# Hybrid attention step on one core: two local projections run in heads 0 and 1 by way of DRAM, and the modulations move to the same heads

## The chip, the cores and the metric

The kernel runs on one core of a Trainium2 chip. The metric is the device time of one execution in microseconds. A core has TensorE (PE; PEld is its weight load), VectorE (DVE), ScalarE (ACT), GpSimd (POOL) and SyncE (SP), which issues the DMAs here. The engines run beside each other and are ordered by semaphores.

## The reference

Two layers act on 1,024 sample tokens and 128 prompt tokens of width 1,024, here 9 tiles of 128 tokens. Each layer is, cut to what matters:

```python
shift, scale, gate = split(silu(c) @ w_ada + b_ada)      # modulation: three parts of 1024
h = layernorm(x) * (1 + scale) + shift
q, k, v, g_att, f, g_f, u, vm, g_m = split(h @ w_in)     # 4 x 512, then 5 x 256 columns
a = softmax(q1 k1) - lam * softmax(q2 k2)                # 4 heads, 1024 queries, 1152 keys
att = rmsnorm(a @ v) * subln_w * silu(g_att)
four = fft2(f per group of 64) @ w_f * silu(g_f)
gmlp = u * (w_s @ layernorm(vm per head of 64) + b_s) * silu(g_m)
x = layernorm(alpha * x + gate * ([att, four, gmlp] @ w_out)) * ln_g + ln_b
```

The prompt's tokens attend to themselves alone, with modulations of their own; their keys and values are outputs too.

## The kernel before, in words

All matrix products take fp32 operands that are split in a high and a low part, so that each product is three matmuls (high x high, high x low, low x high). The normalized, modulated input H stays in SBUF for a whole layer.

**The attention** (`attention`, `Head`) goes through 4 heads of 8 query blocks of 128. A block has two maps; each takes six score matmuls (line 627), the maximum on VectorE (629) and the exponential on ScalarE (631). `softmax_diff` then scales one map on GpSimd (573) and combines both on VectorE into P (574). One block later TensorE transposes P (641), ScalarE and VectorE split it (644, 645), and once per two blocks TensorE multiplies it by V (651, 27 matmuls). `finish_o` normalizes the result by a matmul of squares (583). `prompt` does the same for the 128 prompt tokens of a head in five small pieces between the steps.

**TensorE's order** is written by hand during the attention (`manual_schedule` for PE): the attention is a generator that yields after each piece, and at each yield `fill.fill(FILL[h] * SHARE[step])` takes projection work off a `Stream` until the given debt is used up. Three projection matmuls of 384 columns count 486, two of 256 columns count 218. `fill.until` takes whole projections at once where a head needs them. The other engines' instructions, and all after the attention, are ordered by a planner from the order of the program, with free buffers; work of low priority may run ahead.

**The stream** holds, in this order: the 16 units of the four heads (K, V, Q, G each; 128 columns by 24 x 3 matmuls of 384 tokens, `mm_dims`, line 375), of which each loads the next one's weights when its first chunk is done; then `local_vm`, `local_u` (u and g_m) and `local_f`, with 256 columns token by token (`mm_tok`, lines 390 and 395). `local_vm` normalizes its result in place: statistics per token and head (778, 779), a power on GpSimd (781), and 36 scalings a layer (785). What the stream still holds at the end of the attention is done at once; then the projection g_f runs beside `local_gmlp` and `fourier_prepare`, followed by `local_fourier` and `out_proj`.

**The modulations** (`mods`): a part multiplies 8 weight tiles with the condition's values and sums up in two accumulators, on VectorE (185, 190) and for three products on ScalarE and GpSimd (187, 188); 8 matmuls sum over the partitions (196). Layer 0's own shift and scale come before its attention. Beside layer 0's attention run its gate and layer 1's shift and scale, beside layer 1's its gate, by `extra.fill(MFILL)` at each step of heads 2 and 3; a part yields nine times 1,000.

**Buffers.** `W` has three tiles for split weights; `wr` two raw tiles that weights and modulations share; `z` three for rotated projections and the like; `mm` two PSUM banks for projections and prompt pieces; `S` two groups of three banks for scores, transposes and values.

## Time and profile before

| | us |
|---|---|
| median of 3 runs (lowest, highest) | 1443.29 (1438.05, 1448.58) |
| the profiled execution | 1441.99 |
| its span | 1440.1 |
| PE busy | 1339.8 (93%) |
| PEld busy | 1234.9 (86%) |
| DVE busy | 908.6 (63%) |
| POOL busy | 794.7 (55%) |
| ACT busy | 746.5 (52%) |

The mean granted clock is 0.982 of full speed. The span runs from the first to the last instruction. Busy times are sums over the span; TensorE's matmuls are pipelined, with modelled ends. DMA moves 114.43 MB, 79 GB/s over the span. In layer 0 the attention goes from 102 to 571 us, in layer 1 from 808 to 1258 us.

### The profile page before, as it was taken

How to read it: one execution, taken by the hardware profiler on the slowest of the kernel's cores; microseconds unless marked ns; L12 is line 12 of the kernel's file. 1: busy time of each engine (PE TensorE's matmuls, PEld its weight loads, DVE VectorE, ACT ScalarE, POOL GpSimd, SP SyncE). 2: the span in 40 equal slices, each digit the busy share in tenths (PEclk: the TensorE clock that was granted, in tenths of full speed). 3: DMA queues.
4: the chain of work that ended last, by engine and by line, in shares of the span. 5: the costliest groups of instructions: out<-in, count | busy, mean ns of one | idle time of the engine just before them, and what ended most of it. 6: DMA issues, size and time to landing. Idle time of an engine off the chain costs nothing. (4 is left out here: it accounts for less than half of the span.)

```text
span 1440.1 us, 21257 instructions
## 1 busy us (share of the span) xinstructions
PE 1339.8 (93%) x8248; PEld 1234.9 (86%) x8248; DVE 908.6 (63%) x1351; ACT 746.5 (52%) x1380; POOL 794.7 (55%) x723
## 2 busy tenths in 40 slices
PE   7899998889899899999998989989799999999997
PEld 3688998879689899987888989988789999998786
DVE  5446667786877856345785565668775684435576
ACT  3466566556454345353565665665565544435320
POOL 3275667576563445236777675575674343533752
PEclk9999999999999999999999999999999999999999
DMA  9310011211221221354341100112110010126432
GB/s 340 142 34 31 19 34 49 76 61 32 87 66 32 88 66 56 100 191 149 124 151 54 51 20 31 48 37 88 32 58 10 30 47 30 42 80 224 152 130 84
DMA packets 56157, 114.43 MB, mean 79 GB/s; under 512 B 4972, under 2 KB 32492, under 8 KB 55928
## 3 DMA queue, kind: packets, MB, share of 16 engines
q1 hardware_dynamic: 56056, 113.07, 23.7%
q8 instruction: 65, 1.06, 0.3%
q14 instruction: 36, 0.29, 0.1%
HBM read 95.47 MB, written 17.58 MB: 79 GB/s over the span
## 5 line engine op out<-in xcount | busy, mean ns | idle before, releaser
L375 PE MATMUL z<-H,w 128*128 128x384 f32 x2520 | 498.7, 344 | 25.5 <-DVE V L495 5.8
L375 PEld LDWEIGHTS z<-H,w 128*128 128x128 f32 x2520 | 443.1, 192 | 32.5 <-ACT vT L481 4.9
L631 ACT ACTIVATE P<-S,nm 128x1152 f32<-128x1152 f32 x128 | 156.4, 1222 | 121.2 <-DVE nm L629 114.5
L629 DVE TENSOR_REDUCE nm<-S 128x1 f32<-128x1152 f32 x128 | 172.3, 1349 | 41.6 <-PE S L627 40.8
L390 PE MATMUL zt<-whi,H 128*128 128x256 f32 x1152 | 158.9, 286 | 5.8 <-ACT ug L756 4.3
L390 PEld LDWEIGHTS zt<-whi,H 128*128 128x128 f32 x1152 | 147.2, 192 | 8.5 <-ACT ug L756 5.0
L573 POOL TENSOR_SCALAR P<-P,rz,neglam 128x1152 f32<-128x1152 f32 x64 | 86.8, 1356 | 101.8 <-DVE rz L572 90.4
L574 DVE SCALAR_TENSOR_TENSOR P<-P,rz 128x1152 f32<-128x1152 f32 x64 | 105.0, 1641 | 42.6 <-POOL P L573 42.6
L619 POOL TENSOR_TENSOR qlo<-qr,Q 64x128 fp32r<-64x128 f32 x128 | 81.5, 642 | 85.8 <-PE S L627 80.2
L356 POOL TENSOR_TENSOR w<-wraw,w 128x1024 fp32r<-128x1024 f32 x36 | 89.6, 2490 | 65.0 <-ACT w L355 64.3
L627 PE MATMUL S<-K,Q 128*128 128x384 f32 x384 | 93.7, 353 | 20.0 <-DVE a L645 9.3
L651 PE MATMUL pv<-a,V 128*128 128x256 f32 x864 | 109.3, 283 | 3.1 <-ACT P L631 3.1
L651 PEld LDWEIGHTS pv<-a,V 128*128 128x128 f32 x864 | 106.5, 191 | 5.1 <-ACT P L631 5.1
L645 DVE TENSOR_TENSOR a<-T,a 128x1152 fp32r<-128x1152 f32 x64 | 86.6, 1352 | 38.1 <-ACT a L644 38.0
L627 PEld LDWEIGHTS S<-K,Q 128*128 128x128 f32 x384 | 68.0, 195 | 28.5 <-DVE a L645 10.9
L627 PE MATMUL S<-K,qlo 128*128 128x384 f32 x384 | 90.1, 343 | 0.0
L1002 PE MATMUL y<-wob,mx 128*128 128x512 f32 (+1 forms) x342 | 87.0, 381 | 1.9 <-DVE rr L1004 1.9
L644 ACT ACTIVATE a<-T 128x1152 fp32r<-128x1152 f32 x64 | 72.3, 1130 | 28.7 <-PE T L641 28.4
L395 PE MATMUL zt<-wlo,H 128*128 128x256 f32 x576 | 82.7, 284 | 1.1 <-POOL wlo L356 1.1
L1002 PE MATMUL y<-wo,mx 128*128 128x512 f32 (+1 forms) x342 | 80.5, 378 | 0.0
L641 PE MATMUL T<-cs,P 128*128 128x128 f32 x576 | 73.6, 273 | 3.8 <-ACT P L631 3.8
L395 PEld LDWEIGHTS zt<-wlo,H 128*128 128x128 f32 x576 | 75.0, 191 | 1.5 <-POOL wlo L356 1.5
(219 smaller groups left out, 2388.3 us busy)
## 6 DMA issues: line engine op xcount, KB each, us to landing
wraw<-in_w_in_dram SPq DMA_DIRECT2D x52, 512.0 KB, 3.3
wada<-in_w_ada_dram SPq DMA_DIRECT2D x32, 512.0 KB, 3.6
wa<-in_w_ada_dram SPq DMA_DIRECT2D x8, 1024.0 KB, 12.3
woraw<-in_w_out_dram SPq DMA_DIRECT2D x16, 512.0 KB, 3.9
mr<-mix SPq DMA_DIRECT2D x18, 384.0 KB, 3.3
mix<-gs SPq DMA_DIRECT2D x8, 576.0 KB, 3.9
x<-rr SPq DMA_DIRECT2D x9, 512.0 KB, 3.3
xr<-x SPq DMA_DIRECT2D x9, 512.0 KB, 5.2
```

Of the source, the lines that this page charges most:

```text
L356: eng.tensor_tensor(lo, raw, f(hi), op=ALU.subtract)
L375: pe.matmul(z, lhsT=w[:, a, kt, :], rhs=Hc[c][:, b, kt, :], start=n == 0, stop=n == 23)
L390: pe.matmul(z[:, i, :], lhsT=Hc[c][:, a, kt, o:o + 128], rhs=w[0][:, kt, :], start=n == 0, stop=False)
L395: pe.matmul(z[:, i, :], lhsT=Hc[c][:, 0, kt, o:o + 128], rhs=w[1][:, kt, :], start=False, stop=kt == KT - 1)
L573: pool.tensor_scalar(p2, p2, rz[:, 1:2], neglam[:, l:l + 1], op0=ALU.mult, op1=ALU.mult)
L574: return dve.scalar_tensor_tensor(p1, p1, rz[:, 0:1], p2, op0=ALU.mult, op1=ALU.add)
L627: pe.matmul(S[:, n, :CH], lhsT=q, rhs=K[:, m, n * CH:(n + 1) * CH], start=e == 0, stop=e == 1)
L629: dve.tensor_reduce(nm, S[:, :, :CH], axis=AX.XY, op=ALU.max, negate=True)
L631: act.activation(P.rearrange("p (c k) -> p c k", c=3), S[:, :, :CH], AF.Exp, bias=nm, accum_out=zz[:, m:m + 1])
L645: dve.tensor_tensor(lo, T[:, :, 0:3], f(hi), op=ALU.subtract)
L651: pe.matmul(pv[:, 0, :], lhsT=self.V[:, a, kt, :], rhs=self.A[:, b, kt, :], start=kt == 0 and e == 0, stop=kt == 8 and e == 2)
L1002: pe.matmul(z, lhsT=mx[:, a, k, :], rhs=wo[kt][b][:, ns], start=i == 0, stop=i == 23)
```

## The change

The stream gets another order: `local_f` stands behind head 1's K, V and Q, `local_vm` behind head 2's, and `local_u` is last. The results of f and of vm, the latter normalized, are stored to DRAM from small tiles of the `z` buffers, and two new steps load them behind the last unit, into the tiles where they were computed before. Weights are loaded ahead only as far as the unit before f or vm; f and vm, their own weights loaded, ask for the unit behind them. FILL has other values. The modulations' steps lie in heads 0 and 1 instead of 2 and 3, and what is left of them is done at head 2's first step. The prompt's sum of squares gets a PSUM bank of its own.

```diff
-MHEAD = 2
-MFILL = 450
+MHEADS = (0, 1)
+MFILL = 480
...
-FILL = [1600, 1500, 1500, 2950]
+FILL = [2450, 2450, 1600, 1700]
...
-X_TAGS = {..., "z": (..., "Pp", "modacc"), ...
+X_TAGS = {..., "z": (..., "Pp", "modacc", "vg", "fg"), ...
...
+    f_d = [dr.tile([128, NT, 256], F32, name=f"f_{l}") for l in range(L)]
+    vm_d = [dr.tile([128, NT, 256], F32, name=f"vm_{l}") for l in range(L)]
...
-        def gen(self, which, together=False, chunks=(0, 1, 2)):
+        def gen(self, which, together=False, chunks=(0, 1, 2), ahead=99):
...
-                            self.load_to(g[-1] + 1)
+                            self.load_to(min(g[-1] + 1, ahead))
...
-            pv = psM((128, 2, 128), "pvp")
-            pe.matmul(pv[:, 0], lhsT=self.vp, rhs=aT, start=True, stop=True)
-            sq = square_o(pv[:, 0], 128)
+            pv = psM((128, 128), "pvp")
+            pe.matmul(pv, lhsT=self.vp, rhs=aT, start=True, stop=True)
+            sq = square_o(pv, 128)
             yield 0.5 * PACE
-            finish_o(l, pv[:, 0], pv[:, 1], sq, 128, self.gs, slice(SEQ_S, TOK))
+            finish_o(l, pv, psM((128, 128), "msp"), sq, 128, self.gs, slice(SEQ_S, TOK))
...
-    def local_vm(l):
-        vm = res["vm", l] = tB("K", [128, NT, 256], "vm", F32)
+    def local_vm(l, then):
         w = load_w256(l, U_VM)
+        then()
         for ts in TG:
             z = yield from mm_tok(w, ts)
             n = len(ts) * H
-            v = vm[:, ts[0]:ts[-1] + 1]
+            v = tX([128, 2, 256], "vg")[:, :len(ts)]
             act.activation(v, z, AF.Copy)
...
-
-    def local_f(l):
+            sp.dma_start(vm_d[l][:, ts[0]:ts[-1] + 1], v)
+
+    def load_vm(l):
+        vm = res["vm", l] = tB("K", [128, NT, 256], "vm", F32)
+        sp.dma_start(vm, vm_d[l])
+        yield 0
+
+    def load_f(l):
         ff = [tX((128, 4, 256), "ff") for _ in range(2)]
         fp = [small([128, 128], n, 2) for n in ("vp", "kp")]
+        for i in range(2):
+            sp.dma_start(ff[i], f_d[l][:, 4 * i:4 * i + 4])
+            sp.dma_start(fp[i], f_d[l][:, 8, i * 128:(i + 1) * 128])
         res["f", l] = ff, fp
+        yield 0
+
+    def local_f(l, then):
         w = load_w256(l, U_F)
+        then()
         for ts in TG:
             z = yield from mm_tok(w, ts)
-            t = ts[0] % 4
-            if ts[0] == 8:
-                for j in range(2):
-                    act.activation(fp[j], z[:, 0, j * 128:(j + 1) * 128], AF.Copy)
-            else:
-                act.activation(ff[ts[0] // 4][:, t:t + 2], z, AF.Copy)
+            fg = tX([128, 2, 256], "fg")[:, :len(ts)]
+            act.activation(fg, z, AF.Copy)
+            sp.dma_start(f_d[l][:, ts[0]:ts[-1] + 1], fg)
...
-        fill = Stream(proj.gen(range(0, 3), together=True, chunks=(0, 1, 2) if l else (2,)), proj.gen(range(3, 4 * H)),
-                      local_vm(l), local_u(l), local_f(l))
+        fill = Stream(proj.gen(range(0, 3), together=True, chunks=(0, 1, 2) if l else (2,)),
+                      proj.gen(range(3, 7), ahead=6), local_f(l, lambda: proj.load_to(7)),
+                      proj.gen(range(7, 11), ahead=10), local_vm(l, lambda: proj.load_to(11)),
+                      proj.gen(range(11, 4 * H)), load_vm(l), load_f(l), local_u(l))
...
                 fill.fill(FILL[h] * SHARE[step])
-                if h >= MHEAD:
+                if h in MHEADS:
                     extra.fill(MFILL)
+                else:
+                    extra.drain()
```

## Rows read from the trace of the kernel before

**Rows 1.** Page, part 1: busy time and share of the span of each engine

```profile
PE 1339.8 (93%) x8248; PEld 1234.9 (86%) x8248; DVE 908.6 (63%) x1351; ACT 746.5 (52%) x1380; POOL 794.7 (55%) x723
```

**Rows 2.** Windows cut by head: length, PE, PEld, DVE, ACT, POOL busy, PEclk, DMA, GB/s

```profile
102.03:196.80 94.77, 90.43 (x554) 87.35 (x554) 60.52 (x74) 57.12 (x111) 60.37 (x63) 0.98 0.09 31
196.80:300.26 103.46, 94.94 (x591) 91.82 (x591) 75.03 (x87) 63.95 (x122) 65.84 (x65) 0.98 0.20 60
300.26:416.84 116.58, 102.24 (x600) 94.90 (x600) 87.75 (x94) 66.16 (x124) 72.17 (x69) 0.96 0.18 58
416.84:571.00 154.16, 146.33 (x1095) 141.59 (x1094) 111.41 (x204) 72.61 (x126) 74.79 (x60) 0.98 0.19 60
571.00:808.30 237.30, 226.03 (x1214) 198.69 (x1213) 131.54 (x213) 123.45 (x236) 149.06 (x117) 0.99 0.37 122
808.30:903.00 94.70, 90.36 (x553) 87.25 (x552) 60.57 (x74) 57.12 (x111) 60.30 (x63) 0.98 0.10 31
903.00:1006.50 103.50, 95.08 (x592) 91.80 (x592) 75.04 (x88) 63.92 (x122) 65.97 (x65) 0.98 0.19 60
1006.50:1115.40 108.90, 98.45 (x600) 92.48 (x599) 73.45 (x85) 63.60 (x122) 67.30 (x69) 0.98 0.10 33
1115.40:1258.20 142.80, 138.79 (x1079) 137.41 (x1078) 87.26 (x185) 69.30 (x123) 59.36 (x55) 1.00 0.11 35
1258.20:1440.10 181.90, 170.45 (x945) 150.76 (x943) 102.09 (x156) 59.77 (x99) 80.45 (x61) 0.99 0.39 134
```

**Rows 3.** Chain of waits in layer 1: start us, us, what

```profile
1037.76 1.04 PE S L627 x6
...
1072.24 3.59 PE mres L196 x8
...
1094.94 2.08 PE z L375 x12
...
1146.57 0.96 PE zt L395 x8
```

**Rows 4.** Timeline of PE, layer 1's head 1: start us, us, ..., [idle before]

```profile
957.44 0.45 PE L674 MATMUL atp<-cs,Pp 128*128 128x128 f32 x1 [2.31 <-DVE rz L572]
...
978.50 0.81 PE L627 MATMUL S<-K,Q 128*128 128x384 f32 x3 [2.45 <-ACT msq L587]
```

**Rows 5.** Groups by line, modulations: busy, mean ns, idle before

```profile
L185 DVE TENSOR_SCALAR macc<-wada,csil 128x1024 f32<-128x1024 f32 x8 | 5.7, 746 | 1.4 <-DMA wada<-in_w_ada_dram 1.2 <-PE mres L196 0.2
...
L187 ACT ACTIVATE wada<-wada,csil 128x1024 f32<-128x1024 f32 x12 | 13.8, 1151 | 9.0 <-DVE macc L190 8.7 <-issue 0.3
...
L188 POOL TENSOR_TENSOR macc<-macc,wada 128x1024 f32<-128x1024 f32 x12 | 29.9, 2489 | 5.8 <-ACT wada L187 5.8
...
L190 DVE SCALAR_TENSOR_TENSOR macc<-wada,csil,macc 128x1024 f32<-128x1024 f32 x44 | 67.3, 1551 | 10.8 <-DMA wada<-in_w_ada_dram 10.6
```

**Rows 6.** Groups by line, the normalization of vm

```profile
L778 DVE BATCH_NORM_STATS2 b<-vm 128x6 f32<-128x64 f32 x72 | 10.7, 206 | 4.8 <-ACT vm L773 4.8
...
L785 DVE TENSOR_SCALAR vm<-vm,mvv,rsv 128x64 f32<-128x64 f32 x72 | 24.5, 411 | 3.0 <-POOL rsv L781 3.0
```

**Rows 7.** Timeline, layer 1's head 2

```profile
1020.14 2.35 POOL L188 TENSOR_TENSOR macc<-macc,wada 128x1024 f32<-128x1024 f32 x1
...
1020.21 3.49 DVE L574 SCALAR_TENSOR_TENSOR P<-P,rz 128x1152 f32<-128x1152 f32 x1 [1.69 <-POOL P L573]
...
1025.02 0.95 PE L627 MATMUL S<-K,Q 128*128 128x384 f32 x3 [4.74 <-DVE a L645]
```

**Rows 8.** Line 574: duration ns min/median/max

```profile
L574 DVE SCALAR_TENSOR_TENSOR P<-P,rz x64: 1379/1419/3540, 111.7 to 1240.0; 128x1152 f32<-128x1152 f32 x64
```

**Rows 9.** DMA issues: KB each, median us to landing

```profile
mix<-gs SPq DMA_DIRECT2D x8, 576.0 KB, 3.9
```

**Rows 10.** Timeline of DVE behind layer 1's attention

```profile
1260.78 2.88 DVE L834 TENSOR_TENSOR vr<-vm,vr 128x1152 fp32r<-128x1152 f32 x1 [2.37 <-ACT vr L833]
```

More of the change, by code (lines that the diff above doesn't have):

```diff
@@ L44 @@
 NEARLY = 6
-FILL = [1600, 1500, 1500, 2950]
+FILL = [2450, 2450, 1600, 1700]
 U_Q, U_K, U_V, U_G, U_F, U_GF, U_U, U_VM, U_GM = 0, 4, 8, 12, 16, 18, 20, 22, 24
-X_TAGS = {"wr": ("wraw", "woraw", "wada", "tabr", "mr", "ba"), "z": ("zz", "sh", "gt", "vT", "gmt", "gmg", "fot", "vs", "bd", "pqp", "ws", "kc", "vc", "Pp", "modacc"), "Q": ("Q", "bdr", "wsr", "h32"),
+X_TAGS = {"wr": ("wraw", "woraw", "wada", "tabr", "mr", "ba"), "z": ("zz", "sh", "gt", "vT", "gmt", "gmg", "fot", "vs", "bd", "pqp", "ws", "kc", "vc", "Pp", "modacc", "vg", "fg"), "Q": ("Q", "bdr", "wsr", "h32"),
           "sq": ("sq", "wft", "dftp", "msq", "bds", "cb")}
```

## The prediction

> **What bounds the kernel now.** I read the page's busy times first, then the busy time cut at the first score matmul of each head, then the chain and the engines' own order inside two heads. TensorE is busy 93% of the span and no other engine more than 63% [rows 1]: only time that TensorE loses can be won. The cut shows where. What a head loses I take as length minus PE busy, plus (1 - PEclk) x length: the granted clock has two levels, 2.4 GHz and half of it, so 0.98 over a window means that 2% of its length was lost at the low level. By that sum layer 0's heads lose 6.2, 10.6, 19.0 and 10.9 us, layer 1's 6.2, 10.5, 12.6 and 4.0; together 46.7 and 33.3 us, 80 in all [rows 2]. The stages between and behind the attentions (237.3 and 181.9 us) run nearly dense.
>
> Two patterns matter. Without modulations, loss falls as projection work per step grows: 10.5 us in head 1 (FILL 1500), 4.0 in layer 1's head 3 (2950). With modulations it rises: layer 0's head 2 loses 8.4 more than its head 1, head 3 loses 6.9 more than layer 1's, and layer 1's head 2 loses 2.1 more than its head 1 [rows 2]. That is 15.3 us for three parts and 2.1 for one.
>
> **The prices of TensorE's work.** From the chain: 12 projection matmuls of 384 columns take 2.08 us (0.173 each), 8 of the token-major ones 0.96 (0.12 each), the six score matmuls 1.04, the eight that close a modulation part 3.59 [rows 3]. None of these counts changes. What changes is their order, so the whole effect is in lost time.
>
> **The projections.** f and vm are 9 tokens x 24 matmuls x 0.12 = 25.9 us each per layer. Counted from the yields, a head has 26, 28, 28 and 30 shares of FILL. Before, that hands out 41.6, 42.0, 42.0 and 88.5 thousand; after, 63.7, 68.6, 44.8 and 51.0. Following the generators, 158 token-major matmuls of f and 200 of f and vm enter heads 0 and 1, the rest of vm lies in head 2, and head 3 keeps G3 and u. Behind the attention 70 matmuls remain instead of 158: 10.6 us of TensorE work move ahead of its end.
>
> What head 1 loses shows what the longer steps are worth: 2.31 us before the prompt's transpose, which waits for VectorE's reciprocal, 2.45 before a score matmul that waits for a bank still read by ScalarE [rows 4]. A step of fill precedes each, and it grows by some 1 us. So at 2450 head 1's loss lies between 4.0 (the 2950 row) and 10.5 (the 1500 row); 2950 is nearer, and I take 5.0. Head 0: 6.2 becomes 3.0 by the same ratio. Head 2 at 1600 keeps 9.5 of 10.5. Head 3 at 1700 goes from 4.0 to 9.0, just under the 1500 row: the gain of two heads is mostly paid back there. Together 26.5 a layer against 6.2 + 10.5 + 10.5 + 4.0 = 31.2.
>
> **The modulations.** One part is 2 starts of 0.75, 11 VectorE multiply-adds of 1.55 (together 18.5 us), and three ScalarE products with GpSimd adds of 2.49 [rows 5]. The step's share (480 against 450) hardly changes the pace: a part takes 17 steps, its closing matmuls stand in TensorE's order at the 17th step, the 36th, and the start of head 2. VectorE is busy 60.5 + 75.0 us in layer 0's heads 0 and 1 [rows 2], some 14 of it already modulation work run ahead (two starts and eight multiply-adds lie before head 2); with three parts (57 with their last adds) and two thirds of vm's normalization (for both layers 24.5 scaling and 10.7 statistics, with the short aggregates about 20 a layer [rows 6]) it has some 192 us in about 250, or 77%, where layer 0's head 2 now has 75%. So VectorE is as full as where the loss is greatest, but the steps are half as long again. The bounds per part are 2.1 (layer 1) and 5.1 (15.3 / 3); I take 4.0 for each of layer 0's three, and 2.1 in layer 1. If a closing matmul finds the sums late, the attention's matmuls stand behind it, for TensorE's order is fixed.
>
> One row speaks against the move. While a GpSimd add of a modulation ran (2.35 us), VectorE's P took 3.49 us and the next score matmul waited 4.74 [rows 7]; P's shortest is 1.38 and its median 1.42 [rows 8]. The Trainium skill has the rule, in Advanced Engine Details and Errata, GPSIMD Details: the Pool engine shares a read and a write interface with VectorE and conflicts with its instructions of two SBUF inputs. The trace agrees, 3.49 us against 1.42. By the rule each of the twelve adds can hold P by 2.07 us, 25 us in all, where my sum holds 14.1 for everything that the parts do; that is the first rival.
>
> **DRAM.** Each layer gains ten stores and five loads on SP's queue: 9 x 128 x 256 floats twice out and back, 4.7 MB. The nearest row, a 576 KB store, lands in 3.9 us [rows 9], and the data are wanted a head or more later. A store waits for ScalarE or the scaling, and weight loads queue behind it; they are issued a unit ahead. Between 0 and +4 us a layer, taken 0. The scratch tiles take one or two of three shared buffers while no unit is rotating: 0 to +3, taken 0. Loading no further than the unit before f or vm could expose one load each (0 to +4); the 26 us of f and vm cover the next unit's. The evacuations are the same operations.
>
> **The prompt's second bank.** The sum-of-squares matmul now needs a second bank of a pair that a projection shares, so it waits until VectorE has read the first. In exchange that read no longer follows the matmul. Between are a step of fill and VectorE's longest instruction shown, 3.49 us [rows 7]: once per head, from about -1 to +1.7; taken 0.
>
> **The end of the attention.** The 8.4 us of projection that remain must cover the splitting of vm, which after layer 1's attention ended (1258.2) ran until 1263.66 [rows 10], 5.5 us. That still fits; what no longer fits are u's last gate chain and slower loads. 0 to +5 a layer, taken +1.
>
> **The sum.** Layer 0: 26.5 + 12.0 = 38.5 against 46.7, -8.2. Layer 1: 26.5 + 2.1 = 28.6 against 33.3, -4.7. Ends +2. Together -11 us from the profiled execution's 1441.99, or 1431; that execution stood 1.3 under the median, so **1432**.
>
> **Rivals.**
> *The modulations collide (slower).* In layer 0's heads 0 and 1 GpSimd is busy 64% before anything is added [rows 2], and three parts in two heads meet the softmax more often. If each add holds P by 2.07 us on TensorE's path, and the last product and add (1.15 + 2.40) stand before the closing matmuls, a part costs 9.8 instead of my mean 3.5. Four make 39 against 14, so +25: 1457. It breaks even near 6.3 a part. Against it: longer steps absorb a 2 us delay that a 1500 step did not. Chance 0.20.
>
> *Longer steps close the gaps (a larger gain).* Head 0 at 1600 loses 6.2, head 1 at 1500 loses 10.5 [rows 2]. If that is a knee and not only head 0's fewer steps, heads 2 and 3 lose 6.5 and 6.0, heads 0 and 1 2.0 and 4.0, and a part 2.1: layer 0 24.8, layer 1 20.6, and with the ends -33: 1410. Against it: head 0 has no older head's values in its first steps. Chance 0.26.
>
> *Loss only moves.* If it falls on a straight line from 10.5 at 1500 to 4.0 at 2950, the heads give 28.3 instead of 31.2 a layer, the parts cost what they did (17.4), and the ends take 2: -4, 1439. Chance 0.12.
>
> **How the numbers follow.** The forecast has 0.42, with its own range 1422 to 1442 from the bounds above. One per cent, about what can be told from no change here, is 14.4 us: below 1429 is faster. A third of the forecast's chance lies there, 0.15, and with the larger gain 0.41 is faster; the rest, 0.27, and the moved loss give 0.39 the same; 0.20 slower. The range 1409 to 1454 takes in the larger gain's own figure and most of the collision.
>
> **What would show it.** Layer 0's heads should last 118, 133, 115 and 107 us (before 94.8, 103.5, 116.6, 154.2), layer 1's 116, 122, 112 and 107, each stage behind an attention about 10 us less. The prompt's wait should be under 1.5 us in heads 0 and 1. P above 3 us beside a modulation add, with score matmuls waiting over 4 us there, would show the first rival; closing matmuls that wait for the sums likewise. Heads 2 and 3 under 7 us of loss would show the second. The forecast is wrong if head 3's loss stays near 4, or if heads 0 and 1 lose over 12 in layer 1, where one part runs.

## The result: 2.5% slower, and where the time stands in the profile after

The changed kernel takes 1477.65 us (median of 4 runs, 1475.95 to 1479.98) against 1443.56 for the kernel before on the same chip: ratio 1.0249, 95% interval 1.0223 to 1.0275 (the two medians by themselves give 1.0236, inside it). The forecast was 1432, with a range up to 1454. The profiled execution took 1475.95 with a span of 1474.2, 34.1 more than the span of before. The mean granted clock is 0.972 (0.982 before).

The page's busy times, as in [rows 1]: the work is the same (8,248 matmuls), but PE's time rose by 8.4 us, while the mean granted clock fell from 0.982 to 0.972.

```profile
PE 1348.2 (91%) x8248; PEld 1240.8 (84%) x8248; DVE 912.6 (62%) x1351; ACT 745.4 (51%) x1378; POOL 793.7 (54%) x723
```

The windows of the kernel after, cut as in [rows 2] (length, then PE, PEld, DVE, ACT and POOL busy, PEclk, DMA share, GB/s): layer 0's four heads, the stage behind its attention, then the same for layer 1.

```profile
103.61:231.41 127.80, 115.03 (x716) 108.62 (x715) 91.65 (x99) 65.51 (x123) 79.54 (x67) 0.96 0.25 78
231.41:369.50 138.09, 123.37 (x807) 116.99 (x808) 99.86 (x142) 72.71 (x133) 84.62 (x73) 0.98 0.24 76
369.50:486.99 117.49, 108.83 (x686) 102.59 (x684) 78.91 (x151) 62.53 (x118) 66.39 (x69) 0.99 0.17 59
486.99:589.32 102.33, 99.22 (x747) 97.56 (x747) 59.21 (x66) 58.01 (x105) 42.41 (x44) 1.00 0.10 33
589.32:827.35 238.03, 216.02 (x1097) 189.95 (x1096) 139.18 (x216) 124.60 (x238) 151.93 (x120) 0.95 0.36 118
827.35:952.39 125.04, 114.33 (x717) 108.42 (x716) 79.78 (x90) 65.09 (x124) 72.31 (x66) 0.96 0.20 65
952.39:1073.60 121.21, 116.16 (x792) 114.38 (x791) 67.91 (x126) 65.53 (x125) 66.40 (x69) 1.00 0.14 46
1073.60:1184.67 111.07, 103.35 (x669) 99.71 (x668) 74.22 (x143) 62.40 (x118) 64.32 (x69) 1.00 0.14 48
1184.67:1288.23 103.56, 99.56 (x747) 97.66 (x747) 61.40 (x66) 58.11 (x105) 42.09 (x44) 1.00 0.10 32
1288.23:1474.17 185.94, 165.51 (x844) 144.37 (x843) 110.46 (x158) 60.84 (x102) 83.05 (x64) 0.94 0.38 129
```

A stage's length has to be set against the work that moved. Per layer 100 token-major matmuls left the stage behind the attention and entered the heads, 100 x 0.12 = 12.0 us [rows 3]; in layer 0 the closing of one modulation part moved the same way (3.6 us and its transposes, some 4).

| | before | after | change | work moved | lost time: change | forecast |
|---|---|---|---|---|---|---|
| up to the attention | 102.0 | 103.6 | +1.6 | 0 | +1.6 | 0 |
| layer 0, heads | 469.0 | 485.7 | +16.7 | +16.0 | +0.7 | -8.2 |
| layer 1, heads | 449.9 | 460.9 | +11.0 | +12.0 | -1.0 | -4.7 |
| layer 0, stage behind | 237.3 | 238.0 | +0.7 | -16.0 | +16.7 | +1 |
| layer 1, stage behind | 181.9 | 185.9 | +4.0 | -12.0 | +16.0 | +1 |

The heads only miss the gain that was forecast, 12.9 us; the loss is not there, where the prediction looked for gain and for harm. Each stage behind an attention has 12 to 16 us less to do and is no shorter: TensorE's idle time there went from 11.3 to 22.0 and from 11.5 to 20.4, and PEclk from 0.99 to 0.95 and 0.94, so part of what is left runs at the low level (1.2 GHz): PE is busy 6.0 and 7.1 us longer there than the moved work leaves.

**What holds the stage.** The timeline of the kernel after, behind layer 1's attention (end 1288.23). Columns: start, duration, engine and line, what ended the idle time. `ug` is u, multiplied by its gate, `ws` the raw spatial weights of gmlp, `wsr` their split, `sg` gmlp's products, `taba` the next table.

```profile
1300.54 1.24 DVE L408 TENSOR_TENSOR gmg<-zt,gmt 128x512 f32<-128x512 f32 x2
...
1301.31 1.29 POOL L766 TENSOR_TENSOR ug<-ug,gmg 128x512 f32<-128x512 f32 x1 [1.14 <-DVE gmg L408]
...
1302.62 0.81 SPq L821 DMA_DIRECT2D ws<-in_wsT_dram  x1
1304.87 0.74 POOL L766 TENSOR_TENSOR ug<-ug,gmg 128x256 f32<-128x256 f32 x1
...
1305.63 0.33 SPq L821 DMA_DIRECT2D ws<-in_wsT_dram  x1
...
1309.33 0.74 POOL L846 TENSOR_TENSOR wsr<-ws,wsr 128x256 fp32r<-128x256 f32 x1 [2.56 <-ACT wsr L845]
1309.57 0.68 PE L832 MATMUL sg<-vr,wsr 128*128 128x320 f32 x4
...
1330.57 0.52 PE L832 MATMUL sg<-vr,wsr 128*128 128x256 f32 x3
...
1331.13 2.01 ACT L845 ACTIVATE taba<-tabr 128x1024 fp32r<-128x1024 f32 x2 [1.71 <-PE sg L832]
```

This is a hand-over of buffers. The multiply of u's gate ends at 1302.60, and the load of `ws` is issued at 1302.62; the next ends at 1305.61, and the second load goes at 1305.63. `ws` and the gate's temporaries (gmt, gmg) share the three `z` buffers. So the load goes out 14.4 us after the attention's end, the products run from 21.3 to 42.9 us after it, and only when they have read `vr` (the split of vm) is the buffer free that `taba` shares with it.

The same places in the kernel before, whose attention ended at 1258.22:

```profile
1251.22 0.37 SPq L809 DMA_DIRECT2D ws<-in_wsT_dram  x1
...
1300.67 0.52 PE L820 MATMUL sg<-vr,wsr 128*128 128x256 f32 x3
...
1301.23 2.01 ACT L833 ACTIVATE taba<-tabr 128x1024 fp32r<-128x1024 f32 x2 [1.02 <-PE sg L820]
```

There u stood ahead of f: its gate was done early, `ws` was loaded 7.0 us before the attention's end, and what the products waited for was the projection that was still to do. `taba` started 43.0 us behind the attention before and 42.9 after; from there to the end it takes 138.9 us before and 143.0 after. The remainder shrank, and the load that f used to cover came out from under it. That the load is the cause, and not only late, is tested by a_ws below.

### The profile page after: what moved, and what is told of

The parts are those of the page before. It is cut to its first block, busy times and chain, and to the rows that moved or that the text cites. A ratio compares the mean times of both kernels' runs of the same rounds, so it can differ in the third digit from the quotient of the medians.

```text
span 1474.2 us, 21366 instructions
## 1 busy us (share of the span) xinstructions
PE 1348.2 (91%) x8248; PEld 1240.8 (84%) x8248; DVE 912.6 (62%) x1351; ACT 745.4 (51%) x1378; POOL 793.7 (54%) x723
## 4 chain that ended last, share of the span: by engine, by line
PE 49%; DVE 19%; ACT 9%; POOL 7%; DMA 6%; issue 5%; SPq 0%; DVEq 0%; POOLq 0%; ACTq 0%
PE z L377 16%; PE y L1014 9%; PE zt L392 5%; PE S L629 5%; PE pv L653 5%; DVE macc L192 4%; ACT P L633 3%; PE zt L397 3%; PE T L643 3%; DVE nm L631 2%; DMA wada<-in_w_ada_dram 2%; DVE P L576 2%; DMA woraw<-in_w_out_dram 2%; POOL K L431 1%; POOL P L575 1%
## 5 line engine op out<-in xcount | busy, mean ns | idle before, releaser
L377 PEld LDWEIGHTS z<-H,w 128*128 128x128 f32 x2520 | 447.1, 194 | 53.2 <-ACT Pp L671 23.6
L631 DVE TENSOR_REDUCE nm<-S 128x1 f32<-128x1152 f32 x128 | 172.7, 1350 | 32.7 <-PE S L629 32.1
L653 PEld LDWEIGHTS pv<-a,V 128*128 128x128 f32 x864 | 106.4, 191 | 11.6 <-ACT P L633 8.3
L629 PE MATMUL S<-K,Q 128*128 128x384 f32 x384 | 90.6, 344 | 10.3 <-DVE a L647 4.3
L192 DVE SCALAR_TENSOR_TENSOR macc<-wada,csil,macc 128x1024 f32<-128x1024 f32 x44 | 69.6, 1605 | 15.8 <-DMA wada<-in_w_ada_dram 15.8
L629 PEld LDWEIGHTS S<-K,Q 128*128 128x128 f32 x384 | 65.8, 190 | 14.4 <-DVE a L647 6.3
## 6 DMA issues: line engine op xcount, KB each, us to landing
wa<-in_w_ada_dram SPq DMA_DIRECT2D x8, 1024.0 KB, 10.7
```

What stands on the lines that cost most here:

```text
L192: dve.scalar_tensor_tensor(acc[c], w, k, acc[c], op0=ALU.mult, op1=ALU.add)
L377: pe.matmul(z, lhsT=w[:, a, kt, :], rhs=Hc[c][:, b, kt, :], start=n == 0, stop=n == 23)
L629: pe.matmul(S[:, n, :CH], lhsT=q, rhs=K[:, m, n * CH:(n + 1) * CH], start=e == 0, stop=e == 1)
L631: dve.tensor_reduce(nm, S[:, :, :CH], axis=AX.XY, op=ALU.max, negate=True)
L653: pe.matmul(pv[:, 0, :], lhsT=self.V[:, a, kt, :], rhs=self.A[:, b, kt, :], start=kt == 0 and e == 0, stop=kt == 8 and e == 2)
```

## The experiments

Where an expectation names a theory by a letter, it is one of these. **A**: behind the attention there is a fixed chain, so work done earlier is never given back. **A2**: u is last, so its gate is wanted at once. **B**: the modulations beside the softmax cost the time. **C**: DRAM and the stream's order. **D**: the shorter remainder uncovers a fixed chain. **E**: g_f's projection stands in TensorE's order ahead of gmlp's products. **F**: the load of `ws` waits for `z` buffers that u's gate holds. **G**: the products' results wait for the gate itself. **H**: longer steps close nothing.

All runs at a glance (ratio to the kernel before on the same chip):

| run | median us | ratio, 95% interval |
|---|---|---|
| b_tail3300n | 1438.55 | 0.9993 (0.9974 to 1.0013) |
| a_tail1350 | 1473.19 | 1.0216 (1.0187 to 1.0246) |
| a_tail2250 | 1476.62 | 1.0253 (1.0226 to 1.0280) |
| a_flast | 1476.44 | 1.0246 (1.0221 to 1.0272) |
| a_gf_late | 1474.24 | 1.0224 (1.0189 to 1.0259) |
| a_ws | 1450.29 | 1.0087 (1.0064 to 1.0111) |
| a_mods23 | 1471.04 | 1.0209 (1.0190 to 1.0228) |
| b_mods01 | 1455.26 | 1.0103 (1.0082 to 1.0124) |
| a_flast_mods23 | 1464.76 | 1.0166 (1.0129 to 1.0203) |
| b_best | 1448.23 | 1.0066 (1.0047 to 1.0086) |
| b_mod1 | 1408.64 | 0.9791 (0.9761 to 0.9821) |
| a_mod1 | 1434.52 | 0.9966 (0.9946 to 0.9986) |
| a_ws_mod1 | 1415.55 | 0.9830 (0.9803 to 0.9856) |
| b_nopool | 1433.54 | 0.9927 (0.9898 to 0.9956) |
| b_tail_nopool | 1431.05 | 0.9917 (0.9893 to 0.9942) |
| a_nopool | 1455.93 | 1.0105 (1.0068 to 1.0142) |
| a_ws_mods23 | 1458.53 | 1.0111 (1.0085 to 1.0138) |
| a_ws_nopool | 1444.68 | 1.0027 (1.0013 to 1.0042) |

### The stage behind the attention

**b_tail3300n**: the kernel before, with as little left behind the attention as after the change.

```diff
-FILL = [1600, 1500, 1500, 2950]
+FILL = [1600, 1500, 1500, 3300]
-MFILL = 450
+MFILL = 520
```

> The kernel before with FILL 3300 in head 3 instead of 2950 (and MFILL 520 instead of 450, so that the last modulation still ends before f begins). Counted from the yields, 62 matmuls of f remain behind the attention instead of 158, 11.5 us per layer, and nothing else moves. Theory A (the stage behind the attention is bound by a chain that starts when the attention ends, so work taken out of it shortens it by nothing): both attentions 11 us longer, the stages behind them as long as before (237 and 182 us, within 3), in all 1443 + 20 = 1463. Theory B (the modulations in the heads of the dense softmax cost the time): no change, 1440 to 1447. Theory C (the DRAM loads and the new order of the stream delay what follows the attention): no change either, since neither is here.

Measured: the same time. The windows of its two stages:

```profile
585.10:804.22 219.12, 208.31 (x1103) 184.75 (x1103) 130.49 (x210) 120.41 (x232) 145.10 (x115) 0.99 0.36 125
1263.22:1434.12 170.90, 159.03 (x850) 139.45 (x849) 104.55 (x155) 57.34 (x96) 79.41 (x60) 0.99 0.41 140
```

With 90 token-major matmuls left instead of 184 the stages are 18.2 and 11.0 us shorter than [rows 2], and PEclk stays at 0.99. The 11.0 is the price of the matmuls (94 x 0.12 = 11.3); in layer 0 the closing of a modulation part moved ahead too, with MFILL at 520. A remainder of this size uncovers nothing by itself: A and D fall. What differs from the changed kernel is what the remainder holds, f here and u there; here `ws` went out 21.2 us before the end of layer 1's attention.

**a_tail1350** and **a_tail2250**: the changed kernel with more of u left behind the attention (176 matmuls), and with nothing left.

```diff
-FILL = [2450, 2450, 1600, 1700]
+FILL = [2450, 2450, 1600, 1350]     # a_tail1350; 2250 in a_tail2250
```

> The changed kernel with FILL 1350 in head 3 instead of 1700: 166 matmuls of g_m remain behind the attention instead of 70, as many as the kernel before had of f. Theory A: head 3 is 11 us shorter in each layer, the stages behind keep their 238 and 186 us within 3, in all 1478 - 21 = 1457. Theory B: no change, 1478, each stage behind 11 us longer. Theory C: no change, or slower.

> The changed kernel with FILL 2250 in head 3 instead of 1700, so that nothing of u remains behind the attention. Theory A2: head 3 grows by the 70 matmuls that moved, some 9 us a layer, and the stages behind shrink by 15 to 20, as the gate is ready when they begin: 1455 to 1465. Theory D: the stages stay at 238 and 186 and the heads grow: 1495. Theory B: about 1478.

Neither moves the time by more than half a per cent. But the two show the coupling: at 1350 the load of `ws` goes out 23.4 us behind layer 1's attention, the last product starts at 50.0 and the stage lasts 188.4; at 2250 they are -12.1, 30.0 and 167.8. At 1350 both loads of `ws` again go out at the end of a gate multiply (23.4 and 26.5). At 2250 the stages are 16.6 and 18.1 us shorter, as A2 had it, for 10 us of work; but PE still idles 23.6 and 19.0 us there, so an early load alone does not make a stage dense when nothing is left to cover it. The heads pay the gain back: layer 1's head 3 lasts 119.7 instead of 103.6, 16 us for 10 us of work moved in.

**a_gf_late**: the products' order against g_f's.

```diff
-        fill.fill(1000)
         while fill.gens:
-            post.fill(700)
+            post.fill(1400)
             fill.fill(1500)
```

> The changed kernel with the projection of g_f given out half as fast beside the gmlp products (no 1000 at first, 1400 of the gmlp's steps for 1500 of the projection). Theory A2: the products wait for u's gate, not for their turn: the stages behind the attention 0 to 4 us shorter, 1470 to 1478. Theory E (the projection of g_f stands in front of the gmlp products in TensorE's order): 10 to 15 us shorter each, 1450 to 1458.

The last product now starts 33.6 us behind layer 1's attention instead of 42.6 and `taba` at 34.0, but g_f's projection ends later (51.7 instead of 44.6) and the first DFT product comes at 51.5 instead of 44.5: stages of 234.5 and 184.7, no gain that can be told. E falls as the cause.

**a_flast**: f last and in its own tiles, as before; only vm goes by way of DRAM.

```diff
...                                                 # local_f as in the kernel before
+                      proj.gen(range(3, 11), ahead=10), local_vm(l, lambda: proj.load_to(11)),
+                      proj.gen(range(11, 4 * H)), load_vm(l), local_u(l), local_f(l))
```

> The changed kernel with f alone put back to the end of the stream and into its tiles, without DRAM; vm, the modulations, the prompt's bank and FILL stay as changed. Some 70 matmuls still remain behind the attention, of f instead of u's gate. Theory A2 (what the stream ends with decides: u's gate is wanted at once by the gmlp products, f only later, so with u last the stage behind the attention begins with a wait for the gate, and cover is used up early): the stages behind the attention fall to 219 and 171 us, as with FILL 3300 in the kernel before, the heads stay within 6 us in sum, in all 1444. Theory B (the modulations beside the softmax): 1470 to 1478. Theory D (the shorter remainder uncovers a fixed chain, whatever the remainder is): 1472 to 1480, stages of 238 and 186.

The total did not move, and I had taken that as evidence against u's place until the stages were read: `ws` goes out 9.9 us before the attention's end, PE's idle time there falls from 22.0 and 20.4 to 13.3 and 11.6 us, and the stages (233.5 and 182.4, with 176 matmuls left) are as dense as before. The heads lost it again: with 11 us less work a layer in them they last 7.2 us longer over both layers, and layer 0's head 1 takes 151.5 us with 18.6 idle; why is open. Two effects cancelled in one number.

**a_ws**: one name moved from one pool of buffers to another, nothing else.

```diff
-..."z": (..., "vs", "bd", "pqp", "ws", "kc", ...), ... "sq": ("sq", "wft", "dftp", "msq", "bds", "cb")}
+..."z": (..., "vs", "bd", "pqp", "kc", ...), ... "sq": ("sq", "wft", "dftp", "msq", "bds", "cb", "ws")}
```

> The changed kernel with the gmlp's raw weights (ws) in the three buffers of sq instead of the three of z, and nothing else. Theory F (with u last, its gate's temporaries hold all z buffers, so the load of ws is issued only 14 us behind the attention and the gmlp products start at 21): ws is issued by 5 us, the products start at 11 to 15 us and end 7 to 10 us earlier, and both stages behind the attention are shorter by that: 1458 to 1464. Theory G (the products' results wait for the gate itself, whose last multiplication starts 16.6 us behind the attention): at most 4 us a stage, 1470 to 1478.

Measured: 1450.29, ratio 1.0087; of the 2.5% that the change cost, 1.6 are gone (23 us). The windows of its two stages, and the timeline behind layer 1's attention, which ends at 1277.65:

```profile
592.08:817.13 225.05, 209.67 (x1097) 185.71 (x1096) 135.88 (x216) 124.41 (x238) 151.25 (x120) 0.98 0.37 125
1277.65:1452.29 174.64, 161.20 (x844) 141.09 (x843) 107.08 (x158) 60.28 (x102) 83.58 (x64) 0.97 0.40 137
```

```profile
1280.60 0.38 SPq L821 DMA_DIRECT2D ws<-in_wsT_dram  x1
...
1288.23 0.69 PE L832 MATMUL sg<-vr,wsr 128*128 128x320 f32 x4
...
1309.76 0.52 PE L832 MATMUL sg<-vr,wsr 128*128 128x256 f32 x3
...
1310.39 2.00 ACT L845 ACTIVATE taba<-tabr 128x1024 fp32r<-128x1024 f32 x2
```

The load goes out 2.9 us behind the attention instead of 14.4, `taba` starts at 32.7 instead of 42.9, and the stages are 13.0 and 11.3 us shorter with the same work, more than the 7 to 10 that F had expected. F is shown. G, which allowed 4 us a stage, falls.

### The modulations

**b_mods01** puts them alone where the change puts them; **a_mods23** and **a_flast_mods23** put them back in the changed kernel and in a_flast.

```diff
-                if h >= MHEAD:                    # b_mods01, MFILL 480
+                if h in (0, 1):
                     extra.fill(MFILL)
+                else:
+                    extra.drain()
```

```diff
-MHEADS = (0, 1)                                    # a_mods23; MFILL 480 in a_flast_mods23
-MFILL = 480
+MHEADS = (2, 3)
+MFILL = 450
-                else:
-                    extra.drain()
-    ... load_vm(l), load_f(l), local_u(l))         # a_mods23 only
+    ... load_vm(l), local_u(l), load_f(l))
```

> The kernel before with the modulations alone moved, to heads 0 and 1 at 480 a step. Theory B: 20 to 35 us slower, 1463 to 1478, layer 0's heads 0 and 1 longer by that. Theory A: 1438 to 1452, heads 0 and 1 longer by 10 to 20 us and heads 2 and 3 shorter by 10 to 15.

> The changed kernel with the modulations back in heads 2 and 3 at 450 a step (f is then loaded behind u, since both want the same buffers). Theory B: 20 to 35 us faster, 1443 to 1458, heads 0 shorter by 10 in both layers. Theory A: heads 0 and 1 shorter, heads 2 and 3 longer by as much: within 8 us of 1478, the stages behind as long as in the changed kernel; and in layer 1, where a single part moves, the 5 us wait of head 0 for the prompt's exponential stays.

> As the changed kernel with f last, and the modulations back in heads 2 and 3 at 480 a step. Theory A2: stages of 219 and 171 us; the modulations' place is worth 4 to 8 us, as with the changed kernel: 1436 to 1442. Theory B: 10 us or more under the run with f last alone.

At steps of 1500 the move costs 1.03%, between what A and B expected. In the changed order undoing it gives back 0.4%, at the edge of the noise, and in a_flast 0.8% (11.7 us, as B asked there; A2's 1436 to 1442 was a miss). So B is not the main cause, but the modulations' place is a second, smaller one. In b_mods01 it stands in layer 0 alone: its heads take 490.7 us instead of 469.0, layer 1's 441.7 instead of 449.9. The longer steps take some of it up: by the heads' lengths four parts in heads 0 and 1 cost 52.1 us at the old FILL (b_mods01 against b_mod1 below) and 34.2 at 2450 (the changed kernel against a_mod1), each read from one execution.

In the changed kernel one place of the cost is a wait: TensorE's next projection chunk for the prompt's exponential on ScalarE, which still reads a bank of `mm`. From the waits of PE, after the change (total us, times, longest):

```profile
PE z L377 <- ACT Pp L671: 22.0, 6, 7.4
```

In a_mods23 the same wait totals 8.4 us with 1.7 the longest (A had it stay at 5 us in layer 1, a miss); in the kernel before the total is 2.8. In b_mods01 this wait is 2.2 us; there the longest is another one, 6.6 us of the prompt's transpose behind VectorE. The longest of the kernel after, from the timeline of layer 0's head 1:

```profile
295.06 2.01 DVE L192 SCALAR_TENSOR_TENSOR macc<-wada,csil,macc 128x1024 f32<-128x1024 f32 x1
...
297.10 0.33 SPq L183 DMA_DIRECT2D wada<-in_w_ada_dram  x1
...
297.50 0.47 ACT L589 ACTIVATE msq<-pv,epsr 128x256 f32<-128x256 f32 x1 [3.00 <-DVE gs L586]
297.52 0.38 SPq L476 DMA_DIRECT2D vc<-in_cv_dram  x1
...
300.91 0.31 ACT L477 ACTIVATE V<-vc 128x128 fp32r<-128x128 f32 x1 [2.05 <-DMA vc<-in_cv_dram]
...
301.98 0.37 ACT L671 ACTIVATE Pp<-sp,nmp 128x128 f32<-128x128 f32 x1 [0.75 <-DVE zz L424]
...
302.49 2.29 PE L377 MATMUL z<-H,w 128*128 128x384 f32 x6 [7.37 <-ACT Pp L671]
```

TensorE stands 7.37 us, and two queues make them. ScalarE first stands 3.00 us for a result of VectorE that comes behind modulation multiply-adds. The last of these ends at 297.07 and frees a `wr` buffer; the next modulation weights are issued at 297.10; the prompt's 64 KB `vc` follows on the same queue at 297.52, and ScalarE stands another 2.05 us for it. After 0.75 more for VectorE the exponential runs.

**b_best**: the kernel before with b_tail3300n's values and layer 1's part from head 0 on.

```diff
-                if h >= MHEAD:
+                if l or h >= MHEAD:
```

> The kernel before with FILL 3300 in head 3, and with layer 1's single modulation part in heads 0 and 1 while layer 0's three stay in heads 2 and 3, at 520 a step. From the runs so far, layer 1's heads lost 8 us less with the part there, and the shorter remainder was worth up to 6 in the profiled execution: 1428 to 1435. If the two don't add, 1436 to 1441.

A miss: the effects were expected to add, and it is slower. Layer 1's head 0 takes 112.6 us instead of 94.7, but heads 1 and 2 give that back (its four heads last 458.9 us, in b_tail3300n 459.0). Most of what b_best loses to b_tail3300n stands in the stage behind layer 0's attention, 228.7 instead of 219.1 us: there seven instructions of layer 1's part, asked for from head 0 on, have run ahead into the stage's last 45 us. That they cost the 9.6 us is not shown.

**b_mod1, a_mod1, a_ws_mod1**: what all parts beside the attention cost. Seven of eight products of a part are left out, so that the sums are short of 7/8 of their terms; an eighth of each part still runs.

```diff
         for kt in range(KT):
+            if kt:
+                yield 1000
+                continue
```

> The kernel before with the same seven of eight products left out. The forecast took 17 us for the parts in heads 2 and 3: 1424 to 1428. If the forecast's heads without parts are right (31.2 us lost per layer here, 26.5 in the changed order), this one loses 5 us a layer more in its heads than the changed kernel with the same edit; if longer steps of fill close nothing (theory H), it loses as much or less.

> The changed kernel without seven of the eight products of each modulation part beside the attention (this leaves 7/8 of their sums out). The forecast's price of the parts in heads 0 and 1 is 14 us: 1464. If they cost 9 to 11 each there (theory B for the heads), 1435 to 1445. What the heads lose then is the price of the order and of FILL alone, against the same edit in the kernel before.

> The changed kernel with ws in the sq buffers and seven of the eight products of each modulation part beside the attention left out (leaves out 7/8 of those sums): the changed order with both causes out of the way, to stand beside the kernel before with the same products left out, 1409 us. If ws and the modulations add: 1434.5 - 27 = 1408, so the order of the stream, with its steps of 2450, is worth nothing, where the forecast had 9.4. If the longer steps do close gaps, as the forecast and the rival of a larger gain have it, and only the stages hid it: 1399 or less. If the late ws was partly the modulations' doing: 1415 to 1425.

Windows of b_mod1: layer 0's four heads, and layer 1's attention as a whole:

```profile
101.27:195.98 94.71, 90.36 (x553) 87.28 (x553) 60.51 (x74) 57.10 (x111) 60.41 (x63) 0.98 0.09 31
195.98:294.54 98.56, 92.77 (x591) 90.34 (x591) 63.35 (x81) 61.49 (x120) 62.34 (x66) 1.00 0.10 31
294.54:394.71 100.17, 96.84 (x600) 90.91 (x600) 68.22 (x83) 62.88 (x121) 58.42 (x65) 1.00 0.11 36
394.71:546.46 151.75, 144.67 (x1095) 140.09 (x1095) 88.27 (x190) 69.31 (x123) 58.56 (x55) 0.99 0.10 34
...
785.55:1220.53 434.98, 417.27 (x2819) 404.39 (x2819) 278.00 (x418) 250.53 (x472) 240.47 (x246) 1.00 0.10 33
```

The same windows of a_mod1:

```profile
102.38:217.91 115.53, 110.24 (x716) 104.95 (x716) 68.02 (x82) 62.28 (x121) 56.95 (x63) 1.00 0.12 40
217.91:345.60 127.69, 122.21 (x809) 117.16 (x807) 71.10 (x131) 65.97 (x125) 66.41 (x69) 0.99 0.12 40
345.60:460.65 115.05, 107.74 (x685) 101.09 (x684) 76.64 (x146) 62.33 (x118) 64.60 (x69) 1.00 0.18 60
460.65:564.24 103.59, 99.55 (x747) 97.65 (x747) 61.45 (x66) 58.10 (x105) 42.14 (x44) 1.00 0.09 32
...
798.61:1249.13 450.52, 429.14 (x2919) 416.71 (x2919) 267.94 (x413) 247.98 (x468) 230.28 (x242) 1.00 0.12 42
```

By the prediction's own sum (length - PE busy + (1 - PEclk) x length) a head without the parts loses 6.2, 5.8, 3.3 and 8.6 us at FILL 1600, 1500, 1500, 2950, and 5.3, 6.8, 7.3 and 4.0 at 2450, 2450, 1600, 1700. These are layer 0's; layer 1's are 4.4, 5.8, 3.6, 4.0 and 4.8, 6.0, 7.5, 3.1. Nothing falls with the length of the step: H stands. In the whole time the parts are worth 2.1% in the kernel before (30 us), 2.8% in the changed one (41) and 2.6% in a_ws (37); the 17 and 14 us of the forecast were far too small. The order of the stream without them and with `ws` mended (a_ws_mod1, 0.9830) is not faster than before without them (b_mod1, 0.9791); the intervals overlap, so no difference is shown, and the 1399 or less that closing gaps would have given did not come. Whether the late `ws` was partly the modulations' doing (1415 to 1425) is not settled by its 1415.55: the two effects added give a ratio of 0.9804, just inside the interval.

**b_nopool, a_nopool, b_tail_nopool, a_ws_nopool**: all sixteen products of a part on VectorE.

```diff
-MODS_POOL = (1, 4, 7)
+MODS_POOL = ()
```

> The kernel before, with the modulations' three GpSimd adds a part (and their ScalarE products) given to VectorE as multiply-adds like the other thirteen. The four parts cost the kernel before 30 us. If the GpSimd adds cost it, by holding VectorE's P (3.5 instead of 1.4 us) and by sums that come late: 1441 - 12 to 16 = about 1427, with heads 2 and 3 of layer 0 each 4 to 6 us shorter and no P of the attention above 2.5 us there. If VectorE's queue costs it, each multiply-add standing in front of the softmax: 12 more of 1.55 us there, 1441 + 6 to 12 = about 1450.

> The changed kernel with the same edit: no modulation product on ScalarE and GpSimd, all sixteen on VectorE. The four parts cost the changed kernel 42 us. If the GpSimd adds cost it: 1477 - 16 to 22 = about 1458, layer 0's heads 0 and 1 together 10 to 14 us shorter. If VectorE's queue costs it: 1477 + 6 to 12 = about 1486.

> The kernel before with FILL of head 3 at 3300, MFILL 520 and no modulation product on GpSimd, a candidate for a version faster than both. With the larger remainder of head 3 alone the time was that of before (0.999). If the GpSimd adds cost: about 1425. If VectorE's queue costs: about 1450, and nothing here is faster than before.

> The changed kernel with both mends: ws in the sq buffers, and no modulation product on GpSimd. The mends gained 27 us and 22 us alone. If they are separate: 1450 - 21 = 1429, level with the kernel before mended in the same way (b_nopool, b_tail_nopool: 1431 to 1434), so the change itself is worth -5 to +1 us once both losses are gone. If half of the gain without the adds was an earlier end of the same stage behind layer 0's attention (that stage 227.4 instead of 238.0, where ws already gives 225.0), only the heads' part is left: 1450 - 10 = 1440. If heads 0 and 1 of layer 0 keep about 125 and 138 us, the two parts' cost there is VectorE's queue and not the adds.

Giving VectorE 12 multiply-adds more makes both kernels faster: 0.7% before, 1.4% after. So the way over ScalarE and GpSimd costs more than 12 multiply-adds on VectorE; the edit takes the ScalarE products away with the adds and does not tell the two apart. P's durations (ns, min/median/max) in the kernel after, in b_nopool and in a_nopool:

```profile
L576 DVE SCALAR_TENSOR_TENSOR P<-P,rz x64: 1377/1418/3540, 120.2 to 1276.3; 128x1152 f32<-128x1152 f32 x64
```

```profile
L574 DVE SCALAR_TENSOR_TENSOR P<-P,rz x64: 1376/1419/2556, 110.8 to 1232.7; 128x1152 f32<-128x1152 f32 x64
```

```profile
L576 DVE SCALAR_TENSOR_TENSOR P<-P,rz x64: 1393/1419/3623, 119.6 to 1256.1; 128x1152 f32<-128x1152 f32 x64
```

Only a small part of this is in the heads, though: they add up to 918.9 us before, 912.8 in b_nopool, 946.6 after and 938.8 in a_nopool, 6.1 and 7.8 us for twelve adds (6.0 and 10.0 in the pairs with b_tail3300n and a_ws). My 10 to 14 us for layer 0's heads 0 and 1 were a miss (2.8), and so were the 4 to 6 us for each of heads 2 and 3 in b_nopool (2.3 and none). In a_ws_nopool layer 0's heads 0 and 1 keep 124.8 and 138.2 us: by the sign set in its expectation, the parts' cost in these heads is VectorE's queue and not the adds. Of a_nopool's gain, 10.6 us stand in the stage behind layer 0's attention (227.4 instead of 238.0). PE idles 16.8 us there instead of 22.0 and PEclk is 0.98 instead of 0.95; why is open, and with `ws` mended it does not come again (224.1 against 225.0).

b_tail_nopool, at 0.9917, is the fastest version of the whole computation here, with b_nopool within its interval. a_ws_nopool, the change with both mends, is at 1.0027: 0.3% slower than before, with an interval that leaves out 1, and 1% behind the kernel before with the one mend that suits it too. The two mends do not add (1429 us expected, 1444.68 measured).

**a_ws_mods23**: both undone at once.

```diff
-..."z": (..., "pqp", "ws", "kc", ...), ... "sq": (..., "bds", "cb")}
+..."z": (..., "pqp", "kc", ...), ... "sq": (..., "bds", "cb", "ws")}
-MHEADS = (0, 1)                                    # and the rest of a_mods23's edit
+MHEADS = (2, 3)
```

> The changed kernel with ws in the sq buffers and the modulations back in heads 2 and 3 (MFILL 450, no drain, load_f behind local_u): what is left of the change is the order of the stream with f and vm by way of DRAM, FILL and the prompt's bank. If the two effects are separate they add: 1450 - 6.6 = 1444, and against before -1 to +5, so that the new order itself is worth nothing. If the load of ws was delayed by the same work as the modulations, one edit contains the other: 1450. If the longer steps of heads 0 and 1 are worth what was forecast (4.7 us a layer) once both others are out of the way: 1434.

A miss: 1458.53, not 1444. Layer 1's stage has a_ws's length (173.6). In layer 0 the rest of u ends 15.5 us behind the attention instead of 10.7 and `ws` goes out at 9.7 instead of 2.9, and the stage is 235.6 (some 4 of the 10.5 us more are the closing of a modulation part). The timeline there:

```profile
594.19 0.41 PE L173 MATMUL modt<-cs,ba 2*128 2x2 f32 x4
...
594.63 0.33 SPq L869 DMA_DIRECT2D tabr<-in_dft_dram  x1
...
595.01 0.42 SPq L821 DMA_DIRECT2D ws<-in_wsT_dram  x1
```

The last modulation part now closes behind the attention. Its sum `ba` lies in a `wr` buffer until 594.60; `tabr`, which shares that pool, is issued at 594.63, and `ws` stands next on SP's queue. So the gain of a_ws hangs on when a buffer comes free, be it one of another pool for a load ahead in the queue.

## Why the prediction was wrong

**The end of the attention** is the step that failed. It was taken at +1 a layer, with bounds 0 to +5, because "the 8.4 us of projection that remain must cover the splitting of vm", 5.5 us. That the split still fits was right. "u's last gate chain" was even named, and given a few microseconds without following what its buffers hold: the stage's head is the load of `ws`, behind the gate in the `z` buffers, then its split, the products, and the one buffer that `vr` and `taba` share. The prediction also had 88 matmuls leave the stage where 100 did. The step cost 16.7 and 16.0 us, so 32.7 instead of 2. a_ws takes most of it away by a buffer alone: there the stages lose 8.5 us more than before in place of 32.7 (399.7 us with 28 us less work, against 419.2).

**The longer steps.** The base was to fall from 31.2 to 26.5 a layer. Without the parts it is 24.0 and 17.7 us before, and 23.4 and 21.4 after (b_mod1, a_mod1). The baseline was wrong, not the value after: head 1's 10.5 us at 1500, which the prediction read as a head without modulations, held the parts' work run ahead. Without it that head is 98.6 us long instead of 103.5 and loses 5.8. The prediction counted this work (eight multiply-adds before head 2) in VectorE's load and forgot it in the baseline. Instead of -9.4 the base changed by +3.1 over both layers; with PEclk in two decimals such a sum is good to some 2 us a layer.

**The modulations** were mis-sized by the same slip: 22.7 us in layer 0 and 15.6 in layer 1 before (forecast 15.3 and 2.1), 24.9 and 11.1 after (12.0 and 2.1), 9 to 10 a part. Their change, -2.3, was forecast as -3.3; that it came out near is luck, as both prices were less than half of the real ones. What it set against the first rival, that longer steps absorb delays, has some support (52.1 against 34.2 us above). The first rival's 9.8 a part was the right price, but the kernel before paid it too, and not by that rival's mechanism: five of the twelve adds lie beside a P of 2.9 us or more, before and after alike, no score matmul waits over 2.5 us in the kernel after where over 4 was the sign, and the way over GpSimd is worth 6 to 10 us for all twelve adds in the heads. The Trainium skill's rule (Advanced Engine Details and Errata, GPSIMD Details), that Pool conflicts with VectorE's instructions of two SBUF inputs, agrees with the traces in kind: P takes up to 3.54 us against 1.42. The rest of a part's price was not split further; the wait behind VectorE's and SP's queues above is one place of it.

**The prompt.** Its own wait in heads 0 and 1 is 1.7 us at the longest where under 1.5 was forecast, but the wait came back on the next projection chunk, 5.05 and 7.37 us. The second bank's matmul waits 1.6 us in all, so that term was right at about 0. **DRAM** at 0 stands: in the kernel after no engine is seen to wait for the loads of f or vm, so the DRAM half of C falls too.

**The head lengths** were forecast as 118, 133, 115, 107 and 116, 122, 112, 107, and are 127.8, 138.1, 117.5, 102.3 and 125.0, 121.2, 111.1, 103.6: where the work went was right, and heads 0 and 1 of layer 0 are 10 and 5 us longer. Both warnings came true: head 3 loses 3.1 and 4.0 us, and layer 1's heads 0 and 1 20.8.

Summed: base +3.1, parts -2.3, ends +32.7, the start +1.6: +35, against the spans' +34.1; the forecast had -11.

## What to carry to other kernels

When work moves ahead of a boundary, list what the work that now stands last holds, buffers of shared pools above all, and which loads of the next stage wait for them; covering time counted in microseconds of work says nothing if its cover starts later. A baseline "without X" must be taken where the trace shows no instruction of X, not where the program schedules none: run-ahead fills the neighbour. And an unchanged total can be two effects that cancel, so read an experiment by stage before letting it strike a theory out.

## What the runs showed of the hardware

In these stages waiting was paid twice. With 10.7 and 9.0 us more idle time the granted clock fell there from 0.99 to 0.95 and 0.94, and PE was busy 6.0 and 7.1 us longer than the moved work leaves: together the 16.7 and 16.0 us. In a_ws, with 15.4 and 13.4 us idle instead of 22.0 and 20.4, the clock is back at 0.98 and 0.97. The prediction's measure, (1 - PEclk) x length, gives 9.5 and 9.4 us for the clock, more than the busy time shows, since it also counts the low level while TensorE is idle.

P is also long beside other GpSimd work than the modulations' adds: without any of them (a_nopool) its longest is still 3.62 us, and of nine executions over 2 us four lie beside the rotation's multiply (line 422), three beside the split of weights (358) and two beside the split of K (431). Taking twelve products off ScalarE and GpSimd was worth 0.7% in the kernel before and 1.4% in the changed one, even at the price of 12 more multiply-adds on VectorE.
